# Dilated attention: the scores of both heads of a pair issued together, on the two halves of the array's rows

## The chip, the cores and the metric

The kernel runs on one core of one Trainium2 chip. Its time is the device time of one execution in microseconds (us). The core's engines are TensorE (PE; its weight loads are listed apart as PEld), VectorE (DVE), ScalarE (ACT), GpSimd (POOL) and SyncE (SP), which issues most of the DMAs.

## What is computed

Two blocks follow each other: one of two layers with two kinds of attention side by side, and one with adaptive norms, grouped attention, pooling, convolution and two mixtures of experts. The change lies in the first block, in its dilated attention: 512 tokens, 8 heads of width 64, three groups with dilations 1, 4 and 16. Shortened:

```python
DIL_PAIRS = ((128, 1), (512, 4), (2048, 16))
...
def banded_attention(q, k, v, half):
...
    s = jnp.einsum('nbqhd,nbkhd->nbhqk', qp, kw).astype(jnp.float32) * (Dh ** -0.5)
    s = jnp.where(valid[None, :, None], s, -jnp.inf)
    m = jnp.max(s, axis=-1, keepdims=True)
    e = jnp.exp(s - m)
    l = jnp.sum(e, axis=-1, keepdims=True)
    o = jnp.einsum('nbhqk,nbkhd->nbqhd', (e / l).astype(v.dtype), vw)
    lse = (m + jnp.log(l))[..., 0]
...
def dilated_attention(dil_qkv, cos, sin):
...
    alpha = jax.nn.softmax(jnp.stack(lses, axis=0), axis=0)
    out = jnp.einsum('gbsh,gbshd->bshd', alpha, jnp.stack(outs, axis=0).astype(jnp.float32))
```

The weighting of the three groups by their log-sums makes this the same as one softmax over all keys of the three groups. The kernel uses that: a row of 512 scores holds 256 columns of group 0 and 128 each of groups 1 and 2, and a mask takes out what doesn't count.

## The kernel before

The first block (`block1_layer`, L451) runs twice, for layers L = 0 and 1. Its attention is cut into 64 **units** per layer, a unit being one head and one quarter of 128 queries: units 0 to 31 are the 8 latent heads ("MLA"), units 32 to 63 the 8 dilated heads, four units to a head. So there are 32 dilated units in each layer, 64 in all, and two heads make a pair of 8 units. `unit(u)` (L892) issues, in this order on PE: `scores(u)`; at every eighth unit `values` of the pair before (L851); and `transposed(u - 2)` (L837), which turns the probabilities of two units ago.

`scores(u)` (L802) takes one PSUM bank from the pool "s", which has two. For a dilated unit it issues four matmuls at L824, each with 64 contraction rows and 32 output partitions (`tile_position=(e * 64, 32 * j)`), and two at L830 and L831 with 64 rows and 128 output partitions. `e` is the head within its pair: head 0 of a pair has its queries and keys on partitions 0 to 63, head 1 on partitions 64 to 127 of the same tiles. All of these are float32, for which the trace shows two matmul records each. Then DVE adds the mask and takes the row minimum (L833, into a `pr` tile, of which there are three), ACT takes the exponential with its sum (L795), and DVE takes the reciprocal and scales (L797, L798). `transposed` brings the result through PE (L844) into a `PT` tile, and `values` multiplies it with V for both heads of the pair, on the two halves of the output partitions (L859 for MLA, L865 and L874 for dilated heads).

Between the units stands other work, the **fill**: `weave` (L440) deals a list of steps out over the eight units of a window by costs that are written beside them. The lists are `fills` (L903); windows 4 to 7 hold the dilated units:

```python
        qk_[1] + gate(1, 1) + wout(1),
        qk_[2] + v1[4:12],
        qk_[3] + ctx[0:2] + w2[0:2] + gate(1, 2),
        w2[2:3] + gate(1, 3) + ctx[2:4] + w2[3:4],
```

A fill step of the projection kind is 24 matmuls of 128x512 (L350 to L352: each product in three terms) whose weights come by DMA, are rounded by ACT (L401) and get their remainder from DVE (L402). Windows 4 to 6 have about one such step per unit. Window 7 has few, so that several units follow each other with nothing between them. `qk_[hp]` are the projections of the pair's queries and keys: each evacuated by ACT (keys at L569), a few rows sent by DMA to be rotated on DVE (L590 to L599) and sent back by GpSimd's DMAs (L601). `wout` adds an output projection into x (L668), `gate` is evacuated at L648 and L649. Beside all this runs the table work of the second block, on DVE alone (L967 and L968), with weights by DMA.

The order on PE and SP is the order of the program; that on DVE, ACT and POOL is set by a scheduler.

Of the kernel before, what the change touches and what calls it, by code (L numbers as in the profile page):

```python
# [21 lines left out]
P = 128  # L22
# [248 lines left out]
class K:  # L271
# [17 lines left out]
    def t(self, shape, tag, bufs, dt=F32):  # L289

        pool = self.sb if tag in ("wraw", "whi", "wlo", "cath", "catl") else self.two if tag == "big" else self.of.get(tag, self.pool)
        return pool.tile(shape, dt, tag=tag, bufs=bufs, name=self.nm(tag))
# [158 lines left out]
def block1_layer(k, L, x, hT):  # L451
    nc, I, t, fm = k.nc, k.I, k.t, k.fm
# [249 lines left out]
    cats, vss, qks, gates, mq, cT, vm = {}, {}, {}, {}, {}, [], []  # L702
# [89 lines left out]
    def softmax(pr, bias, src):  # L792

        l = t([P, 1], "l", 4)
        nc.scalar.activation(pr, src, AF.Exp, scale=-1.0, bias=bias, accum_out=l)  # L795
        rl = t([P, 1], "rl", 4)
        nc.vector.reciprocal(rl, l)  # L797
        nc.vector.tensor_scalar(pr, pr, rl, None, op0=ALU.mult)  # L798

    heads = [Head() for _ in range(16)]  # L800

    def scores(u):  # L802
        h, i = u // 4, u % 4
        hd = heads[h]
        dil, hh = h // 8, h % 8
        e = hh % 2
        rows = slice(e * 64, e * 64 + 64)
        if i == 0:
            hd.pr = {}
        sp = k.bank("s")  # L810
        mn = t([P, 1], "mn", 4)
        cs = slice(i * P, (i + 1) * P)
        if not dil:
            q, kt = mq[hh]
            nc.tensor.matmul(sp, q[:, cs], kt, start=True, stop=True)
            pr = t([P, 512], "pr", 3)
            nc.vector.tensor_reduce(mn, sp, AX.X, ALU.min)
            softmax(pr, mn, sp)
        else:
            qs = qks[hh // 2]  # L820
            q0, q1, q2 = (qs[(0, g)] for g in range(3))
            k0, k1, k2 = (qs[(1, g)] for g in range(3))
            for j in range(4):
                nc.tensor.matmul(  # L824
                    sp[32 * j : 32 * j + 32, 0:256],
                    q0[rows, i * P + 32 * j : i * P + 32 * j + 32],
                    k0[rows, P * j : P * j + 256],
                    start=True, stop=True, tile_position=(e * 64, 32 * j),
                )
            nc.tensor.matmul(sp[:, 256:384], q1[rows, cs], k1[rows, cs], start=True, stop=True)  # L830
            nc.tensor.matmul(sp[:, 384:512], q2[rows, cs], k2[rows, cs], start=True, stop=True)  # L831
            pr = t([P, 512], "pr", 3)
            nc.vector.tensor_tensor_reduce(pr, sp, k.dil_mask[:, i, :], 1.0, 3e38, ALU.add, ALU.min, mn)  # L833
            softmax(pr, mn, pr)
        hd.pr[i] = pr

    def transposed(u):  # L837
        h, i = u // 4, u % 4
        hd = heads[h]
        if i == 0:  # L840
            hd.PT = t([P, 4, 512], "PT", 2)
        pt = k.bank("pt")
        for j in range(4):
            nc.tensor.transpose(pt[:, j * P : (j + 1) * P], hd.pr[i][:, j * P : (j + 1) * P], ident)  # L844
        if h < 8:
            dst = hd.PT[:, :, i * P : (i + 1) * P]
        else:
            dst = hd.PT[:, i, :].rearrange("p (j q) -> p j q", j=4)
        k.copy(dst, pt.rearrange("p (j q) -> p j q", j=4))
# [42 lines left out]
    def unit(u):  # L892
        if u < 64:
            scores(u)
        if u >= 10 and u % 8 == 2:
            values(u // 8 - 1)
        if 2 <= u < 66:
            transposed(u - 2)
# [1090 lines left out]
def body(tc, I, out, stop=None):  # L1989
    nc = tc.nc  # L1990
    with (
# [21 lines left out]
        with k.phase("two"):  # L2013
            k.two = k.pool
            with tc.manual_schedule(engines={mybir.EngineType.PE, mybir.EngineType.SP}):
# [27 lines left out]
                for L in range(2):  # L2043
                    block1_layer(k, L, x, hT)
                    k.late = None
# [37 lines left out]
```

## Time and profile before

| | |
|---|---|
| three runs | 1874.26, 1878.16, 1883.65 us; median 1878.16 us |
| profiled execution | 1880.58 us, of which the span is 1878.8 us |
| PE busy | 1739.2 us (93%) |
| DVE busy | 1350.5 us (72%) |
| ACT busy | 772.9 us (41%) |
| POOL busy | 279.5 us (15%) |
| dilated units in time | first layer 253.7 to 490 us, second layer 758.8 to 992 us from the span's start |
| mean granted clock of PE over the span | 0.96 |

Shares are of the span. Matmul records overlap, since the next one starts before the last has ended: the time that a group of matmuls takes on PE is read from start to start of what follows, not from the sum of its durations.

### The profile page before, as it was taken

What the parts mean: (1) busy time and instruction counts of PE and PEld (TensorE: products, weight loads), DVE (VectorE), ACT (ScalarE), POOL (GpSimd) and SP (SyncE); (2) the same over time, 40 slices, a digit from 0 to 9 for tenths busy, and PEclk for the clock granted to TensorE, in tenths of its full rate; (3) what the DMA queues carried; (4) which work ended last, traced back from release to release, by engine and by line L of the source; (5) the groups of instructions that cost most, each with busy time, mean ns of one, the idle gap of its engine ahead of it and who ended that gap; (6) DMA issues with size and microseconds to landing.
All of it is one profiled execution on the core that took longest, in us unless ns stands there. A gap on an engine that the chain in (4) does not pass through costs nothing. (4 is left out here: it accounts for less than half of the span.)

```text
span 1878.8 us, 25737 instructions
## 1 busy us (share of the span) xinstructions
PE 1739.2 (93%) x9542; PEld 1346.2 (72%) x9542; DVE 1350.5 (72%) x2532; ACT 772.9 (41%) x1345; POOL 279.5 (15%) x242
## 2 busy tenths in 40 slices
PE   7999999999899999999997879996999799969996
PEld 6877777787697767778776857774666587846663
DVE  4577778876546777576566797879887775689874
ACT  4444333334343533333424445553555332135552
POOL 0000000001100000000002353013321121142221
PEclk9999999999999999999998879997999799979998
DMA  5345565654023544554412213136996463169983
GB/s 174 120 138 152 157 201 164 208 165 133 20 72 116 147 143 139 172 161 139 153 56 89 75 55 115 52 144 244 331 347 211 153 229 90 46 230 308 345 297 75
DMA packets 86948, 298.90 MB, mean 159 GB/s; under 512 B 18854, under 2 KB 20694, under 8 KB 78624
## 3 DMA queue, kind: packets, MB, share of 16 engines
q1 hardware_dynamic: 71584, 271.87, 43.8%
q0 software_dynamic: 10704, 19.79, 4.6%
q10 hardware_dynamic: 4528, 5.51, 1.1%
q8 instruction: 78, 1.28, 0.3%
q14 instruction: 54, 0.44, 0.1%
HBM read 280.23 MB, written 24.96 MB: 162 GB/s over the span
## 5 line engine op out<-in xcount | busy, mean ns | idle before, releaser
L401 ACT ACTIVATE whi<-wraw 128x1024 fp32r<-128x1024 f32 (+2 forms) x166 | 171.8, 1037 | 356.7 <-PE psmm L351 240.3
L402 DVE TENSOR_TENSOR wlo<-wraw,whi 128x1024 fp32r<-128x1024 f32 (+3 forms) x165 | 200.9, 1219 | 133.7 <-ACT whi L401 121.0
L350 PE MATMUL psmm<-big,whi 128*128 128x512 f32 x672 | 271.6, 404 | 0.8 <-ACT e L1265 0.8
L351 PE MATMUL psmm<-big,whi 128*128 128x512 f32 x672 | 265.8, 396 | 0.0
L352 PE MATMUL psmm<-big,wlo 128*128 128x512 f32 x672 | 265.6, 395 | 0.0
L968 DVE CUSTOM_DVE_ANT_0 wraw<-wraw,sB 128x1024 f32<-128x1024 f32 x96 | 117.3, 1222 | 73.1 <-DMA wraw<-in_mw_dram 72.6
L350 PE MATMUL psmm<-whi,big 128*128 128x256 f32 (+2 forms) x496 | 165.3, 333 | 1.0 <-ACT big L401 1.0
L351 PE MATMUL psmm<-wlo,big 128*128 128x256 f32 (+2 forms) x496 | 160.7, 324 | 4.7 <-DVE wlo L402 4.7
L352 PE MATMUL psmm<-whi,big 128*128 128x256 f32 (+2 forms) x496 | 160.1, 323 | 2.4 <-DVE big L402 2.3
L352 PEld LDWEIGHTS psmm<-big,wlo 128*128 128x128 f32 x672 | 126.4, 188 | 30.8
L350 PEld LDWEIGHTS psmm<-big,whi 128*128 128x128 f32 x672 | 126.6, 188 | 29.2 <-ACT e L1265 1.0
L351 PEld LDWEIGHTS psmm<-big,whi 128*128 128x128 f32 x672 | 126.7, 189 | 27.8
L1853 PE MATMUL psmm<-wraw,hs 128*128 128x512 f32 x256 | 121.9, 618 | 5.5 <-ACT hs L1845 3.5
L601 POOL DMA_DIRECT2D qk<-rope x40 | 20.4, 512 | 677.9 <-DVE rope L599 239.7
L351 PEld LDWEIGHTS psmm<-wlo,big 128*128 128x128 f32 x496 | 112.2, 226 | 5.8 <-DVE wlo L402 5.6
L352 PEld LDWEIGHTS psmm<-whi,big 128*128 128x128 f32 x496 | 111.5, 225 | 3.2 <-DVE big L402 3.2
L350 PEld LDWEIGHTS psmm<-whi,big 128*128 128x128 f32 x496 | 111.7, 225 | 2.0 <-ACT big L401 1.6
L350 PE MATMUL pss<-whi,xTh 128*128 128x512 f32 x256 | 104.7, 409 | 2.3 <-ACT xTh L401 2.3
L352 PE MATMUL pss<-whi,xTl 128*128 128x512 f32 x256 | 102.2, 399 | 1.7 <-DVE xTl L402 1.7
L351 PE MATMUL pss<-wlo,xTh 128*128 128x512 f32 x256 | 103.3, 404 | 0.0
L844 PEld LDWEIGHTS pspt<-c_ident,pr 128*128 128x128 f32 x512 | 59.3, 143 | 48.4 <-issue 25.5
L402 DVE TENSOR_TENSOR wlo<-bigm,whi 128x1024 fp32r<-128x1024 f32 x64 | 78.0, 1223 | 17.7 <-ACT whi L401 16.2
(386 smaller groups left out, 3733.1 us busy)
## 6 DMA issues: line engine op xcount, KB each, us to landing
wraw<-in_mw_dram SPq DMA_DIRECT2D x96, 512.0 KB, 4.0
big<-in_me_dram SPq DMA_DIRECT2D x32, 1024.0 KB, 9.1
bigm<-in_me_dram SPq DMA_DIRECT2D x32, 1024.0 KB, 6.6
wraw<-in_me_dram SPq DMA_DIRECT2D x64, 512.0 KB, 7.6
wraw<-in_wqk_dram SPq DMA_DIRECT2D x48, 512.0 KB, 3.8
wraw<-in_wv_dram SPq DMA_DIRECT2D x24, 512.0 KB, 4.1
wraw<-in_ow_dram SPq DMA_DIRECT2D x20, 512.0 KB, 3.6
wraw<-in_wg_dram SPq DMA_DIRECT2D x16, 512.0 KB, 3.6
```

Source lines behind the costliest of these rows:

```text
L350: mm(out, lhs[0], rhs[0], start=first, stop=False)
L351: mm(out, lhs[0], rhs[1], start=False, stop=False)
L352: mm(out, lhs[1], rhs[0], start=False, stop=last)
L401: self.nc.scalar.activation(hi, src, AF.Copy)
L402: (sub or self.nc.vector).tensor_tensor(lo, src, hi.bitcast(F32), ALU.subtract)
L601: nc.gpsimd.dma_start(tiles[b][48:80, :], R[b // 4][32 * (b % 4) : 32 * (b % 4) + 32, :])
L844: nc.tensor.transpose(pt[:, j * P : (j + 1) * P], hd.pr[i][:, j * P : (j + 1) * P], ident)
L968: nc.vector.tensor_tensor_reduce(w, w, sB, 1.0, 0.0, ALU.mult, ALU.add, mf[:, j : j + 1])
L1853: nc.tensor.matmul(acc, hs[:, c * P : (c + 1) * P], w[:, c * 512 : (c + 1) * 512], start=c == 0, stop=c == 1)
```

## The change

For the dilated units the order of the units within a pair of heads changes, and the scores of two units are issued as one group. `place(u)` now alternates the heads: the even unit is head 0 of the pair, the odd unit head 1, for the same quarter of the queries. At the even unit `dilated` takes both banks of the pool "s" and issues the matmuls of both heads in turn, head 0 on rows 0 to 63 into one bank, head 1 on rows 64 to 127 into the other. The odd unit issues no score matmuls. Mask, softmax, transposes, values and fill stay with their units. The MLA units are as before.

```diff
+    def place(u):
+
+        return (u // 4, u % 4) if u < 32 else (u // 8 * 2 + u % 2, u % 8 // 2)
+
+    banks = {}
+
+    def dilated(hp, i):
+
+        qs = qks[hp]
+        cs = slice(i * P, (i + 1) * P)
+        pair = [(k.bank("s"), slice(e * 64, e * 64 + 64)) for e in range(2)]
+        for j in range(4):
+            for sp, rows in pair:
+                nc.tensor.matmul(
+                    sp[32 * j : 32 * j + 32, 0:256],
+                    qs[(0, 0)][rows, i * P + 32 * j : i * P + 32 * j + 32],
+                    qs[(1, 0)][rows, P * j : P * j + 256],
+                    start=True, stop=True, tile_position=(rows.start, 32 * j),
+                )
+        for g in (1, 2):
+            for sp, rows in pair:
+                nc.tensor.matmul(sp[:, (g + 1) * P : (g + 2) * P], qs[(0, g)][rows, cs], qs[(1, g)][rows, cs], start=True, stop=True)
+        return [sp for sp, _ in pair]
+
     def scores(u):
-        h, i = u // 4, u % 4
+        h, i = place(u)
...
-            for j in range(4):
-                nc.tensor.matmul(
-                    sp[32 * j : 32 * j + 32, 0:256],
-                    q0[rows, i * P + 32 * j : i * P + 32 * j + 32],
-                    k0[rows, P * j : P * j + 256],
-                    start=True, stop=True, tile_position=(e * 64, 32 * j),
-                )
-            nc.tensor.matmul(sp[:, 256:384], q1[rows, cs], k1[rows, cs], start=True, stop=True)
-            nc.tensor.matmul(sp[:, 384:512], q2[rows, cs], k2[rows, cs], start=True, stop=True)
+            if h % 2 == 0:
+                banks[0], banks[1] = dilated(hh // 2, i)
+            sp = banks[h % 2]
...
     def transposed(u):
-        h, i = u // 4, u % 4
+        h, i = place(u)
```

Lines behind the new functions are 12 higher after the change: L844 becomes L856, L833 becomes L845. The score matmuls of the dilated heads are at L815 (32 output partitions) and L823 (128).

PE's order, before, at the first two dilated units of the first layer (`pss` is a score bank, `psmm` a bank of the fill, `pspt` one of the transposes; the 24 fill matmuls between the units are left out):

```order
L352 MATMUL psmm_2207<-big_77,wlo_2201 128x512
L824 MATMUL pss_2235<-k_443_2032,qk_1538 32x256 x4
L830 MATMUL pss_2235<-qk_1910,qk_1620 128x128
L831 MATMUL pss_2235<-qk_1979,qk_1857 128x128
L844 MATMUL pspt_2250<-c_ident,pr_2154 128x128 x4
...
L824 MATMUL pss_2297<-k_443_2032,qk_1538 32x256 x4
L830 MATMUL pss_2297<-qk_1910,qk_1620 128x128
L831 MATMUL pss_2297<-qk_1979,qk_1857 128x128
L844 MATMUL pspt_2312<-c_ident,pr_2185 128x128 x4
```

PE's order, after, at the same place:

```order
L815 MATMUL pss_2236<-k_443_2032,qk_1538 32x256
L815 MATMUL pss_2237<-k_443_2032,qk_1538 32x256
L815 MATMUL pss_2236<-k_443_2032,qk_1538 32x256
L815 MATMUL pss_2237<-k_443_2032,qk_1538 32x256
...
L823 MATMUL pss_2236<-qk_1910,qk_1620 128x128
L823 MATMUL pss_2237<-qk_1910,qk_1620 128x128
L823 MATMUL pss_2236<-qk_1979,qk_1857 128x128
L823 MATMUL pss_2237<-qk_1979,qk_1857 128x128
L856 MATMUL pspt_2257<-c_ident,pr_2154 128x128 x4
...
L856 MATMUL pspt_2312<-c_ident,pr_2185 128x128 x4
```

The scores of the second unit have moved ahead by one unit, past the transposes and the fill of the first, and stand matmul by matmul between those of the first; the second unit has only its transposes left.

DVE's order, before, at the same two units (`mn` is the row minimum, `wraw` the raw weights of the table work and of the fill):

```order
L833 ISA pr_2243,mn_2236<-pss_2235,dil_mask 128x512
L833 ISA mn_2236 128x1
L649 SCALAR_TENSOR_TENSOR gc_2232<-gc_2232,psmm_2207 128x512
L368 COPY PT_2161<-pspt_2250 128x4x128
L797 RECIPROCAL rl_2247<-l_2245 128x1
...
L833 ISA pr_2305,mn_2298<-pss_2297,dil_mask 128x512
L833 ISA mn_2298 128x1
```

DVE's order, after:

```order
L845 ISA pr_2250,mn_2235<-pss_2236,dil_mask 128x512
L845 ISA mn_2235 128x1
L368 COPY PT_2161<-pspt_2257 128x4x128
L845 ISA pr_2305,mn_2304<-pss_2237,dil_mask 128x512
L845 ISA mn_2304 128x1
L797 RECIPROCAL rl_2254<-l_2252 128x1
```

The mask step of the second unit, which frees the second bank, has moved up to just behind that of the first.

## Rows read from the trace of the kernel before

**Rows 1.** The page's first lines: span, and busy time of each engine.

```profile
span 1878.8 us, 25737 instructions
PE 1739.2 (93%) x9542; PEld 1346.2 (72%) x9542; DVE 1350.5 (72%) x2532; ACT 772.9 (41%) x1345; POOL 279.5 (15%) x242
```

**Rows 2.** Busy time by stretch: dilated units, windows 4 to 6 and 7, each layer.

```profile
core 0: us, PE busy (x) PEld busy (x) DVE busy (x) ACT busy (x) POOL busy (x), PEclk, DMA share, GB/s
253.00:461.00 208.00, 206.68 (x1232) 158.67 (x1234) 161.11 (x295) 73.26 (x122) 15.22 (x26) 1.00 0.59 177
461.00:490.00 29.00, 26.65 (x230) 18.96 (x230) 18.25 (x44) 10.79 (x24) 0.57 (x1) 0.98 0.18 48
758.00:965.00 207.00, 206.25 (x1227) 158.81 (x1226) 133.82 (x257) 70.23 (x121) 10.33 (x23) 1.00 0.50 146
965.00:992.00 27.00, 26.12 (x226) 18.33 (x224) 15.58 (x36) 10.76 (x22) 0.00 (x0) 1.00 0.08 21
```

**Rows 3.** Timeline of PE at a dilated unit: start, us, instruction, [idle before].

```profile
260.52 0.40 PE L351 MATMUL psmm<-big,whi 128*128 128x512 f32 x1
260.75 0.39 PE L352 MATMUL psmm<-big,wlo 128*128 128x512 f32 x1
261.07 0.64 PE L824 MATMUL pss<-k,qk 64*32 64x256 f32 x8
261.64 0.49 PE L830 MATMUL pss<-qk,qk 64*128 64x128 f32 x2
261.96 0.38 PE L831 MATMUL pss<-qk,qk 64*128 64x128 f32 x2
262.28 0.65 PE L844 MATMUL pspt<-c_ident,pr 128*128 128x128 f32 x4
```

**Rows 4.** Score matmuls of all dilated units: count, ns min/median/max, starts; idle before them.

```profile
L824 PE MATMUL pss<-k,qk x512: 372/376/400, 253.7 to 990.1; 64*32 64x256 f32 x171
L830 PE MATMUL pss<-qk,qk x128: 272/322/373, 254.3 to 990.6; 64*128 64x128 f32 x128
L831 PE MATMUL pss<-qk,qk x128: 272/272/272, 254.6 to 990.8; 64*128 64x128 f32 x128
...
  DMA k<-rope: 1.1, 1
```

**Rows 5.** PE timeline: first four column tiles of a unit; the next unit; values on column halves.

```profile
261.07 0.42 PE L824 MATMUL pss<-k,qk 64*32 64x256 f32 x4
...
268.47 0.64 PE L824 MATMUL pss<-k,qk 64*32 64x256 f32 x8
...
269.67 3.65 PE L859 MATMUL psav<-PT,v 128*64 128x512 f32 x16
...
468.48 1.97 PE L865 MATMUL psav<-PT,v 128*64 128x128 f32 x32
```

**Rows 6.** DVE by line, 253 to 461 us: busy us, mean ns, idle before it.

```profile
L968 DVE CUSTOM_DVE_ANT_0 wraw<-wraw,sB 128x1024 f32<-128x1024 f32 x31 | 37.9, 1222 | 19.0 <-DMA wraw<-in_mw_dram 18.7
L402 DVE TENSOR_TENSOR wlo<-wraw,whi 128x1024 fp32r<-128x1024 f32 x26 | 31.8, 1222 | 11.8 <-ACT whi L401 11.8
```

**Rows 7.** Keys of the dilated heads, first layer: evacuations; timeline of POOL and PE.

```profile
L569 ACT ACTIVATE k<-psmm x4: 579/580/587, 231.9 to 445.9; 128x512 f32<-128x512 f32 x4
...
458.71 0.50 POOL L601 DMA_DIRECT2D k<-rope  x1
...
460.93 0.64 PE L824 MATMUL pss<-k,qk 64*32 64x256 f32 x8 [1.14 <-DMA k<-rope]
```

**Rows 8.** Timeline at the end of the first layer's units, DVE and PE.

```profile
486.57 0.69 DVE L833 CUSTOM_DVE_ANT_0 pr<-pss,dil_mask 128x512 f32<-128x512 f32 x1
...
489.73 1.94 PE L844 MATMUL pspt<-c_ident,pr 128*128 128x128 f32 x8 [2.20 <-DVE pr L798]
```

**Rows 9.** Timeline at the end of the second layer's units, DVE.

```profile
988.97 0.69 DVE L833 CUSTOM_DVE_ANT_0 pr<-pss,dil_mask 128x512 f32<-128x512 f32 x1
...
991.40 0.69 DVE L833 CUSTOM_DVE_ANT_0 pr<-pss,dil_mask 128x512 f32<-128x512 f32 x1
```

More of the change, by code (lines that the diff above doesn't have):

```diff
@@ L800, in block1_layer @@
     heads = [Head() for _ in range(16)]
+    def place(u):
[17 more added lines that the diff above has]
+        return [sp for sp, _ in pair]
     def scores(u):
-        h, i = u // 4, u % 4
+        h, i = place(u)
         hd = heads[h]
         dil, hh = h // 8, h % 8
-        e = hh % 2
-        rows = slice(e * 64, e * 64 + 64)
         if i == 0:
             hd.pr = {}
-        sp = k.bank("s")
         mn = t([P, 1], "mn", 4)
-        cs = slice(i * P, (i + 1) * P)
         if not dil:
+            sp = k.bank("s")
             q, kt = mq[hh]
-            nc.tensor.matmul(sp, q[:, cs], kt, start=True, stop=True)
+            nc.tensor.matmul(sp, q[:, i * P : (i + 1) * P], kt, start=True, stop=True)
             pr = t([P, 512], "pr", 3)
@@ L819, in scores @@
         else:
-            qs = qks[hh // 2]
-            q0, q1, q2 = (qs[(0, g)] for g in range(3))
-            k0, k1, k2 = (qs[(1, g)] for g in range(3))
-            for j in range(4):
-                nc.tensor.matmul(
-                    sp[32 * j : 32 * j + 32, 0:256],
-                    q0[rows, i * P + 32 * j : i * P + 32 * j + 32],
-                    k0[rows, P * j : P * j + 256],
-                    start=True, stop=True, tile_position=(e * 64, 32 * j),
-                )
-            nc.tensor.matmul(sp[:, 256:384], q1[rows, cs], k1[rows, cs], start=True, stop=True)
-            nc.tensor.matmul(sp[:, 384:512], q2[rows, cs], k2[rows, cs], start=True, stop=True)
+            if h % 2 == 0:
+                banks[0], banks[1] = dilated(hh // 2, i)
+            sp = banks[h % 2]
             pr = t([P, 512], "pr", 3)
```

## The prediction

> **What bounds the kernel now.** I began with the page's totals: PE is busy for 1739.2 of 1878.8 us [rows 1]. An average over a span proves little, so next I took the stretches in which the changed code runs. In windows 4 to 6 PE is busy for 206.68 of 208 us in the first layer and 206.25 of 207 us in the second, at a granted clock of 1.00 (the upper of its two levels), while DVE has 161.11 and 133.82 us and ACT about 70 [rows 2]. The reader is to see that PE is full there and the next engine is not: a microsecond of PE work removed in these stretches should come off the end. In window 7 PE is still at 26.65 of 29 and 26.12 of 27 us, but the units follow each other closely, so a chain through DVE may take over.
>
> Then the timeline of one unit, to see how long its scores hold PE [rows 3]. The scores begin at 261.07 and the transposes behind them at 262.28: **1.21 us a unit**. That isn't streaming time. Eight records of L824 lie within 0.64 us though each lasts 0.376; the two groups that follow have four records, 0.11 us apart at best (two of L831 within 0.38 us, each 0.272). Most of the rest is waiting at two seams: 0.57 us from the first L824 to L830, and 0.32 us from the first L831 to the transposes. Entering costs something too: the last fill matmul starts 0.32 us ahead of the scores, where fill matmuls start 0.23 us apart, so 0.09 us more. All 64 dilated units look like this: the records of each line have nearly the same minimum, median and maximum over 512, 128 and 128 matmuls [rows 4]. The next unit starts 7.40 us later, so scores are 1.21 of each 7.40 us [rows 3, 5].
>
> **The change, part by part.** No score matmul is added or removed: 8 + 2 + 2 records per unit stay. They are grouped in twos, so 32 groups replace 64.
>
> *Two units before:* 2 x 1.21 + 0.09 for the second entry = 2.51 us. The second unit's transposes will now follow the fill directly, and I take nothing for that.
>
> *One group after:* unknown, because no row shows matmuls on two row halves next to each other. From below: both halves run side by side. The nearest rows are of column tiles. The first four column tiles of a unit, each 0.400 us, all lie within 0.42 us, so they start 0.007 us apart and do run side by side [rows 5]. The values matmuls alternate between two column halves: 32 records of 128 columns take 1.97 us and 16 of 512 columns 3.65 us [rows 5], where one after the other, 0.11 us apart per 128 columns as at L831 [rows 3], they would take 3.5 and 7.0 us. They go two at a time. If row halves do the same, the group is as long as one unit plus a few starts, 1.21 + 0.04 = 1.25 us, and a pair of units gains 2.51 - 1.25 = 1.26, taken as **1.25 us**. From above, as long as the order of column tiles holds: the second half adds its own 0.5 us of column tiles (0.26 from first to last start, and the step of 0.24 to the next) and 4 x 0.11 = 0.44 us, so 1.21 + 0.94 = 2.15 us and a gain of 0.36. Farther out, each L824 matmul of the mixed order runs alone; that is the slow rival. I take the lower bound, because the two halves read different partitions, write different banks, and are as independent as the column halves that the trace shows in twos.
>
> The Trainium skill (TensorEngine Tiling (Array Packing), Key Properties) says that different tiles can load weights and multiply in parallel, and that changing the tiling mode, not the tile alone, drains the engine; by that rule the seams of rows 3 are paid once a group and the gain is the 1.25 us. Its page TensorE: Matmul & The Clock Gate (Part 3) gives 3.07 times for four row tiles, short of four; two tiles at that efficiency, as an estimate, would make the group 2.41/1.53 = 1.6 us and the total about 1854. No row here shows either.
>
> *Where it counts.* Each of windows 4 to 6 has four groups, so 12 in each layer.
> - First layer, windows 4 to 6: window 7 begins with a wait of 1.14 us for the rotated keys. They left PE's banks at 445.9, within the last two units of window 6, and their DMA is issued at 458.71 [rows 7]; this chain doesn't get shorter, so what the last group saves is waited out. 11 x 1.25 = 13.75 us.
> - Second layer, the same windows: the wait for keys occurs once in both layers together [rows 4]; 12 x 1.25 = 15.0 us.
> - Window 7 of each layer has four groups. Three gain 1.25. But a group needs both score banks, and the mask step of the odd unit before it must have freed the second. In windows 4 to 6 the mask steps now stand one behind the other on DVE, a unit of 7 us ahead, so nothing waits. In window 7, where two groups have only values and transposes between them, the odd unit's mask step (0.69 us [rows 8]) needs the `pr` tile that the transposes two units back let go, and PE has only one set of transposes (four records within 0.65 us [rows 3]) to cover it and its signals: I charge 0.5 us once in each layer. 2 x (3.75 - 0.5) = 6.5 us.
> - The last group. In the first layer the last transposes wait 2.20 us for DVE [rows 8], and DVE starts from the fill before, so PE's saving is swallowed: 0. In the second, three mask steps stand in a row behind the last fill, 988.97 to 991.40, about 1.2 us each with what lies between [rows 9]; two remain: 1.25 us.
>
> Sum: 13.75 + 15.0 + 6.5 + 1.25 = **36.5 us**, as much as 29.2 groups in full. Against the profiled execution that is 1880.58 - 36.5 = 1844; that execution stood 2.4 us above the median of 1878.16, so I forecast **1842 us**, 1.9% faster. Costed at nothing: masks, softmax, transposes and copies, which are the same in number and lie under PE's 7 us of fill; without that cover (window 7) they are charged above. Next in line, if PE gives way, is the DVE of the first layer.
>
> **The rivals.**
> - *Weight loads in line.* The halves multiply side by side, but the 128-column weights load one after the other. Column halves can't tell, since a load of 64 columns is half as long. Then the second half's four records add 4 x 0.11 us: a group of 1.69, a gain of 0.82 x 29.2 = 24 us, **1854**.
> - *Halves one after the other* (the change doesn't do what it says): the upper bound of 2.15, only seams saved, 0.36 x 29.2 = 10.5 us, **1868**. For it: no row shows two row halves at once. Against it: rows 5.
> - *DVE takes over in the first layer.* There DVE is busy 161.11 us and idles 19.0 us ahead of the table work, for its weights, and 11.8 us for ACT [rows 2, 6]. If none of that shrinks, 161 + 31 = 192 us is what windows 4 to 6 need, hardly below the 208 - 13.75 = 194 of my forecast; any new stall on DVE, or its order, would give back up to the 13.75 us: **1856**. Against it: ACT waits for PE there, so that part shrinks with PE. The skill's page on tiling (PSUM Bottleneck) names this way out, that tiling doesn't speed up the emptying of banks; by it the time is that of this rival.
> - *Slower: the alternation breaks the column tiles.* If two matmuls on different row halves aren't taken together, e0, e1, e0, e1 means that no two neighbours run side by side. Then 8 matmuls of L815 take two steps of 0.24 us each, 3.84 us in place of 0.48, and the second half adds 0.44 as above: 1.21 + 3.36 + 0.44 = 5.0 us, 2.5 us more than two units before. 32 x 2.5 = 80 us, **1958**. It turns slower from a group of 2.51 us. For it: the order puts every second matmul on the other half. Against it: L859 alternates in just this way between column halves and keeps its twos.
> - *The gain is lost behind*: chains after each layer (norm, weights) don't start earlier. Little speaks for it, as those waits hang on the units' own ends. **1878**.
>
> **How the numbers follow.** Forecast 0.64, with its own range of 1835 to 1849 for the small terms and the spread of the runs; weight loads 0.13; halves in turn 0.07; DVE 0.06; slower 0.05; lost 0.05. A measurement here can tell about 0.5% from no change, 9.4 us, so faster means below 1868.8. Faster: 0.64 + 0.13 + 0.06 + half of 0.07 = 0.86; same: 0.05 + the other half = 0.09; slower 0.05. The range takes in the forecast, the weight loads and DVE, 0.83 in all, with some room: 1832 to 1862.
>
> **What would show it.** In the changed profile a group should hold PE for about 1.25 us from its first L815 to the L856 behind it (1.7: weight loads in line; 2.15: halves in turn; 5: the alternation breaks). The stretches of windows 4 to 6 should shrink by some 14 and 15 us at the same fill. A wait of PE for keys at the first layer's window 7 should be about 2.3 us. Short waits for DVE should stand before a group in window 7 alone. I am wrong if PE shows waits for L845 in windows 4 to 6, if DVE is busy there for over 95%, or if a group is over 2 us.

## The result, and the profile after

The changed kernel takes **1857.26 us** (median of 4 runs, 1853.23 to 1861.11); the kernel before, on the same chip, 1877.49 (4 runs, 1874.26 to 1883.65). The ratio is 0.9888, 95% interval 0.9854 to 0.9922. It is faster by some 20 us: inside the range, in the foretold direction, and little more than half of the 36.5 us of the sum. The profiled execution took 1858.75 us. Its page begins:

```profile
span 1857.0 us, 25754 instructions
PE 1705.9 (92%) x9542; PEld 1334.2 (72%) x9542; DVE 1346.4 (73%) x2532; ACT 770.8 (42%) x1345; POOL 278.2 (15%) x242
```

PE has 33 us less work than in [rows 1], with as many instructions; DVE, ACT and POOL have what they had. The span fell by only 21.8 us. So most of the foretold 36.5 us of PE work went away, and some 11.5 us of it came back as idle time.

First the group itself, PE's timeline at a pair of units in the first layer (start, us, instruction):

```profile
322.43 0.39 PE L352 MATMUL psmm<-whi,catl 128*128 128x512 f32 x1
322.75 0.66 PE L815 MATMUL pss<-k,qk 64*32 64x256 f32 x16
323.34 0.71 PE L823 MATMUL pss<-qk,qk 64*128 64x128 f32 x8
323.99 0.66 PE L856 MATMUL pspt<-c_ident,pr 128*128 128x128 f32 x4
...
330.09 0.60 PE L856 MATMUL pspt<-c_ident,pr 128*128 128x128 f32 x4
```

Sixteen records of L815 begin within the time in which eight did in [rows 3]. From the first to the transposes it is 323.99 - 322.75 = 1.24 us, for two units, where one took 1.21. All 32 groups are like this, but for one in each window 7, which last 2.37 and 1.68 us; in the first of them the trace shows a wait of 0.52 us for a mask step (L845). The second unit has only transposes (330.09).

Then the stretches of [rows 2], cut at the new times (same columns: us, PE, PEld, DVE, ACT and POOL busy, PE's granted clock, DMA):

```profile
253.00:456.00 203.00, 195.19 (x1228) 154.79 (x1226) 160.73 (x295) 71.36 (x121) 16.00 (x26) 0.97 0.59 184
456.00:481.00 25.00, 21.84 (x229) 16.43 (x228) 16.57 (x41) 11.25 (x23) 0.00 (x0) 1.00 0.13 35
748.00:948.00 200.00, 194.09 (x1228) 154.38 (x1226) 132.61 (x257) 69.75 (x121) 10.44 (x23) 0.98 0.50 151
948.00:972.00 24.00, 22.58 (x236) 17.05 (x235) 16.52 (x41) 11.39 (x24) 0.00 (x0) 1.00 0.08 24
```

Where PE idled for 1.3 and 0.75 us in [rows 2], it now idles for 7.8 and 5.9 us, and its granted clock is no longer 1.00. What it waited for, windows 4 to 7 of the first layer and then of the second (us in total, times, longest):

```profile
PE psmm L350 <- DVE x L668: 4.2, 2, 4.0
PE psmm L350 <- DVE gc L649: 3.3, 1, 3.3
PE pspt L856 <- DVE pr L798: 3.0, 1, 3.0
PE pss L815 <- DVE mn L845: 0.5, 1, 0.5
...
PE psmm L350 <- DVE gc L649: 2.7, 1, 2.7
PE psmm L350 <- DVE x L668: 1.6, 1, 1.6
...
PE psmm L351 <- DVE wlo L402: 1.1, 1, 1.1
```

The new ones are those of `psmm`: the fill wants one of its three banks, and DVE hasn't emptied it (L649, a gate; L668, the addition of an output projection). The keys' wait of [rows 7] is gone.

What DVE does ahead of the longest of the first kind, after:

```profile
305.35 0.72 DVE L590 STREAM_SHUFFLE rope<-rope 64x512 f32<-64x512 f32 x1
306.11 1.22 DVE L979 CUSTOM_DVE_ANT_0 v<-wraw,v 128x1024 f32<-128x1024 f32 x1
307.26 0.08 DVE L979 DVE_READ_ACCUMULATOR2_ANT modc<- 128x1 f32 x1
307.26 3.27 DVE L598 TENSOR_TENSOR rope<-rope,v 32x512 f32<-32x512 f32 x4
310.56 0.69 DVE L649 SCALAR_TENSOR_TENSOR gc<-gc,psmm 128x512 f32<-128x512 f32 x1
```

and PE, which has a wait there and then matmuls 0.43 us apart:

```profile
311.30 0.80 PE L350 MATMUL psmm<-whi,cath 128*128 128x512 f32 x1 [3.33 <-DVE gc L649]
311.90 0.63 PE L351 MATMUL psmm<-wlo,cath 128*128 128x512 f32 x1
312.32 0.63 PE L352 MATMUL psmm<-whi,catl 128*128 128x512 f32 x1
```

The same place before, DVE and PE:

```profile
306.73 3.35 DVE L598 TENSOR_TENSOR rope<-rope,v 32x512 f32<-32x512 f32 x4
310.11 0.49 DVE L798 TENSOR_SCALAR pr<-pr,rl 128x512 f32<-128x512 f32 x1
310.51 0.68 DVE L599 TENSOR_TENSOR rope<-rope,rope 64x512 f32<-64x512 f32 x1
311.12 0.67 DVE L649 SCALAR_TENSOR_TENSOR gc<-gc,psmm 128x512 f32<-128x512 f32 x1
...
311.84 0.50 PE L350 MATMUL psmm<-whi,cath 128*128 128x512 f32 x1
```

The gate was emptied half a microsecond *later* there than now, and PE got to its next matmul just as it ended. PE is now ready for it at 311.30 - 3.33 = 307.97, 3.9 us ahead of the start before; DVE isn't. What PE has saved is waited out, and then PE's clock is at the lower of its two levels (1.2 GHz) for a while: 0.51 granted from 310 to 317 us, where 12 fill matmuls go 0.43 us apart and no longer 0.23.

Averages over the stretches hide this. DVE is busy 161 of 208 us in [rows 2]; the piece around this place, before and then after (same columns as above):

```profile
291.00:325.00 34.00, 33.82 (x187) 24.48 (x186) 32.73 (x62) 11.68 (x19) 3.23 (x8) 1.00 0.49 144
```

```profile
288.00:321.00 33.00, 29.67 (x162) 22.67 (x161) 31.36 (x60) 8.86 (x16) 3.23 (x8) 0.90 0.43 133
```

DVE is busy 32.73 of 34 us (96%) before as well, beside a PE that is full. Both engines were full at once there; only PE was made faster.

The other long waits have more than a full DVE behind them. Ahead of the wait of 3.96 us at 448.82, one of the four multiplications took 3.07 us while GpSimd computed the remainder of a weight (L402) beside it, so that the four took 5.31 us and not 3.27:

```profile
442.64 5.31 DVE L598 TENSOR_TENSOR rope<-rope,v 32x512 f32<-32x512 f32 x4
443.59 2.51 POOL L402 TENSOR_TENSOR v<-wraw,v 128x1008 fp32r<-128x1008 f32 x1 [5.16 <-ACT v L401]
```

The same GpSimd step lay beside them before the change too, where they took 4.76 us and PE waited for no fill bank. And ahead of the wait of 2.66 us in the second layer, DVE was not full: it stood idle for 3.07 us, by the trace for the weights of a table step, and then its order put that step and the rotation ahead of the gate:

```profile
797.89 1.23 DVE L980 CUSTOM_DVE_ANT_0 wraw<-wraw,sB 128x1024 f32<-128x1024 f32 x1 [3.07 <-DMA wraw<-in_mw_dram]
799.81 3.37 DVE L598 TENSOR_TENSOR rope<-rope,v 32x512 f32<-32x512 f32 x4
804.95 0.67 DVE L649 SCALAR_TENSOR_TENSOR gc<-gc,psmm 128x512 f32<-128x512 f32 x1
```

### The profile page after: what moved, and what is told of

It reads as the page before. It is cut to its first block, busy times and chain, and to the rows that moved or that the text cites. A ratio compares the mean times of both kernels' runs of the same rounds, so it can differ in the third digit from the quotient of the medians.

```text
span 1857.0 us, 25754 instructions
## 1 busy us (share of the span) xinstructions
PE 1705.9 (92%) x9542; PEld 1334.2 (72%) x9542; DVE 1346.4 (73%) x2532; ACT 770.8 (42%) x1345; POOL 278.2 (15%) x242
## 3 DMA queue, kind: packets, MB, share of 16 engines
q8 instruction: 78, 1.28, 0.3%
## 5 line engine op out<-in xcount | busy, mean ns | idle before, releaser
L401 ACT ACTIVATE whi<-wraw 128x1024 fp32r<-128x1024 f32 (+2 forms) x166 | 171.7, 1036 | 348.1 <-PE psmm L351 241.6
L402 DVE TENSOR_TENSOR wlo<-wraw,whi 128x1024 fp32r<-128x1024 f32 (+3 forms) x165 | 200.9, 1219 | 102.3 <-ACT whi L401 89.6
L856 PEld LDWEIGHTS pspt<-c_ident,pr 128*128 128x128 f32 x512 | 61.3, 143 | 48.2 <-issue 28.9
L402 DVE TENSOR_TENSOR wlo<-bigm,whi 128x1024 fp32r<-128x1024 f32 x64 | 77.9, 1223 | 17.7 <-ACT whi L401 16.2
```

The lines of the kernel that those rows point to most:

```text
L401: self.nc.scalar.activation(hi, src, AF.Copy)
L402: (sub or self.nc.vector).tensor_tensor(lo, src, hi.bitcast(F32), ALU.subtract)
```

## The experiments

**Theory A**, from these rows: in windows 4 to 6 DVE's rotation of queries and keys (L590 to L599, with L598 alone 3.3 us), with table work among it, stood hidden under PE's slower units. Now it is late, PE waits for a fill bank, and the clock falls behind the wait. **Rivals**: the pairing of the score banks makes PE wait (Theory B below); the clock falls by itself (Theory C); the new order of the units costs the time (Rival D). Number 3 asks something else, whether the two halves run side by side only because their matmuls alternate.

**1. The rotation's second step left out.** The kernel leaves out the multiplications of L598, so its queries and keys differ; their values take another path through the experts at the end (1536 matmuls at L1905, on a path that the changed kernel doesn't enter), and its total (4298.81 us) says nothing. Only the stretch up to the end of the dilated units is read.

```diff
-                    for sl, perm in ((slice(0, 32), "p (r l) -> p r l"), (slice(32, 64), "p (r l) -> p l r")):
...
-                            nc.vector.tensor_tensor(d, d, dil_cs[sl, c, :].rearrange(perm, r=4), ALU.mult)
+                    pass
```

> The changed kernel, with the four multiplications of the second rotation step (L598, 4 x 0.82 us of DVE for each pair of heads) left out, so keys and queries of that step are not rotated. Theory A (PE, now ahead, waits for banks of the fill that DVE empties too late, since the rotation stands ahead of the gate's and the output projection's steps in DVE's order, and PE's clock halves after each such wait): the waits of 3.3, 4.0, 2.7 and 1.6 us shrink to under 1 us each, the stretches at half clock behind them go, and of the 17 us lost most come back: 1840 us, 1837 to 1847. Theory B (the two score banks taken together cost the time): nothing changes but the shorter DVE time, 1857. Theory C (the clock falls by itself): the waits go, the half-clock stretches stay, 1846.

PE's waits in windows 4 to 6 of the first layer, and the longest in those of the second:

```profile
PE psmm L350 <- DVE x L665: 0.2, 1, 0.2
...
PE psmm L351 <- DVE wlo L402: 0.4, 1, 0.4
```

No stretch of lower clock is left in either. As a marker behind the units of the second layer I take the second set of four transposes at L414: it starts at 950.65 us, where it is 971.82 in the changed kernel and 994.06 before. So without that work on DVE the dilated windows gain 21 us more, though PE has the same instructions. The clock doesn't fall by itself, and pairing the banks isn't the cause: the groups are still there. But all of L598 went, 11.9 us of DVE's time in the first layer's windows 4 to 6, so it doesn't say what a smaller cut is worth.

**2. The new order alone.** Heads alternate, each unit issues its own scores.

```diff
-        pair = [(k.bank("s"), slice(e * 64, e * 64 + 64)) for e in range(2)]
+        pair = [(k.bank("s"), slice(e * 64, e * 64 + 64))]
...
+            sp = dilated(hh // 2, i, h % 2)
```

> The units of the two heads alternate as in the changed kernel, but each unit issues its own scores, 64 groups of one head as before. Theory A: PE is as slow as before the change, 1.21 us a unit, DVE keeps up, no wait for a bank of the fill over 0.6 us in the dilated windows, 1877 us (1872 to 1882). Rival D (the new order of the units, by the order that the scheduler then gives DVE, causes the waits): waits of 2.7 to 4 us as in the changed kernel, and a time of 1888 or more.

1881.51 us beside 1881.07 of the kernel before, ratio 1.0005 (0.9994 to 1.0017). A unit's scores take 1.21 us as before, and the longest wait for a fill bank is 0.3 us. The order costs nothing; the waits come with the shorter scores.

**3. One half after the other.** The group stays, but all matmuls of head 0 are issued ahead of those of head 1.

```diff
-        for j in range(4):
-            for sp, rows in pair:
+        for sp, rows in pair:
+            for j in range(4):
```

> The changed kernel with the group in another order: all six matmuls' records of head 0 of a kind first, then those of head 1 (four column tiles of head 0, four of head 1, two of head 0, two of head 1). If PE starts matmuls in the program's order and puts only what stands near side by side: the second half's first column tile waits for the first half's last, some 0.25 us, and the four records of each half at the wide matmuls go 0.11 us apart in turn, 0.35 to 0.44 more; a group of 1.8 us and some 0.6 x 29 = 17 us over the changed kernel, 1874. If halves run side by side in any order: a group of 1.24 us and 1857.

```profile
255.22 0.66 PE L815 MATMUL pss<-k,qk 64*32 64x256 f32 x16
255.81 0.72 PE L823 MATMUL pss<-qk,qk 64*128 64x128 f32 x8
256.47 0.33 PE L856 MATMUL pspt<-c_ident,pr 128*128 128x128 f32 x1
```

The group takes 1.25 us, as in the change, and the kernel 1856.46 us, ratio 0.9878 (0.9859 to 0.9896). What I had expected of this order was wrong: the halves run side by side however they are interleaved, so the gain comes from issuing both within one group.

**4. Fill banks first.** DVE is to prefer the gate and the addition to the rotation.

```diff
+            with k.tc.high_priority():
                 nc.vector.scalar_tensor_tensor(sg, sg, 1.0, acc, op0=ALU.add, op1=ALU.mult)
...
+                with k.tc.high_priority():
                     nc.vector.tensor_tensor(xs, acc, xs, ALU.add)
```

> The changed kernel, with the gate's two steps (ACT and DVE) and the output projection's add on DVE at high priority for the scheduler; in DVE's order the gate's step moves up past three of the four L598 multiplications. Nothing is left out. Theory A: the waits of PE shrink by some 2.5 us each, and part of the half-clock stretches go: 1847 us, 1840 to 1852. Theory B or D: 1857.

1855.38 us, ratio 0.987 (0.9851 to 0.9888), some 8 us above what was expected. PE's two longest waits in the first layer's windows 4 to 6 and at the first scores of window 7:

```profile
PE pss L817 <- DMA k<-rope: 6.3, 1, 6.3
PE psmm L350 <- DVE x L670: 1.7, 1, 1.7
```

The waits for banks shrank, and the rotation, pushed back, made the keys late: 6.3 us at window 7. Both chains run through the same DVE, and order alone only trades one wait for the other.

**5. Half of the rotation's second step on GpSimd.**

```diff
-                            nc.vector.tensor_tensor(d, d, dil_cs[sl, c, :].rearrange(perm, r=4), ALU.mult)
+                            (nc.gpsimd if c else nc.vector).tensor_tensor(d, d, dil_cs[sl, c, :].rearrange(perm, r=4), ALU.mult)
```

> The change, with two of the four multiplications of the rotation's second step (L598, c = 1) moved from VectorE to GpSimd, so that VectorE reaches the emptying of TensorE's fill banks (L649, L668) about 1.6 us sooner in each block. Theory A (VectorE's rotation block, no longer covered, makes TensorE wait for a fill bank): the waits of 3.33 and 3.96 us of the first layer and 2.66 and 1.63 us of the second become about 1.7, 2.3, 1.0 and 0; some 6.4 us of waiting less, and one or two of the half-clock stretches with them: 1848 us (1844 to 1852). Rival G: GpSimd slows VectorE's own multiplications while it runs (they took about 1.25 us in place of 0.82 when GpSimd subtracted beside them), so that little is saved: waits within 0.7 us of what they were, 1855 to 1859.

1860.49 us, ratio 0.9891 (0.9861 to 0.9921): nothing gained. DVE and POOL at the place that was shown above:

```profile
306.02 4.20 POOL L598 TENSOR_TENSOR rope<-rope,v 32x512 f32<-32x512 f32 x2 [3.21 <-DVE rope L590]
...
307.09 4.03 DVE L598 TENSOR_TENSOR rope<-rope,v 32x512 f32<-32x512 f32 x2
```

Two multiplications on DVE took 4.03 us beside two on POOL, where four on DVE alone took 3.27. Rival G holds: the block didn't shrink, and PE's wait was 4.23 us. The Trainium skill (SBUF — State Buffer, "SBUF: two separate sides") says that VectorE and GpSimd take turns at a shared pair of ports, whole instructions at a time, when VectorE reads both its inputs from SBUF and GpSimd reads SBUF as well. The trace agrees: GpSimd's shortest multiplication in this run took 1.27 us, so that two of them and the two of VectorE, one after the other, would need some 4.2 us; from 306.02 to 311.12 the four took 5.1.

**6. Table work moved by one window.** In the first layer window 4 carries two steps of the table work per weight tile; here window 5 does.

```diff
-        k.rate = (1, 1, 1, 1, 2 - L, 1, 1, 0)[w]
+        k.rate = (1, 1, 1, 1, 1, 2 - L, 1, 0)[w]
```

> The change, with the table work's double rate in the first layer moved from the fifth window of units to the sixth, so that one L979/L980 pair less stands among VectorE's rotation work at 305 to 312 us. Theory A: the wait of 3.33 us at 311.30 shrinks to under 1.5 us and its half-clock stretch goes, 4 to 6 us less in the first layer; the second layer is as in the change: about 1852 us. Rival: the table work is not part of what VectorE is late by (the rotation alone makes it late), or the next window's bank now waits in its place: 1857 us.

1864.88 us, ratio 0.9935 (0.9906 to 0.9964), slower than the change by the medians, though the two intervals touch. The wait of 3.33 us became 0.8, and two others came in window 5. PE's waits in the first layer's windows 4 to 6:

```profile
PE psmm L350 <- DVE x L668: 5.0, 3, 4.0
PE pss L815 <- DVE mn L845: 3.8, 1, 3.8
PE psmm L351 <- DVE wlo L402: 3.5, 1, 3.5
PE psmm L350 <- DVE gc L649: 0.8, 1, 0.8
```

So the table work is part of what makes DVE late in window 4, and window 5 has no room for it: by the trace window 4 holds 10 table steps here and not 13, window 5 holds 17 and not 12.

The second layer of this run is as in the change and has the same two waits of 2.66 and 1.63 us, but the granted clock stays at 1.00 behind the first (811 to 816 us). Its window 4 is 2.86 us shorter than in the change (65.77 in place of 68.63) and its window 5 is 1.77 us longer (73.23 in place of 71.46), in one execution of each. So in this pair of executions sparing the lower clock was worth 1.1 us over the two windows, and not 2.9.

**7 and 8. The fill reordered; then edits 5, 6 and 7 together.**

```diff
-        qk_[2] + v1[4:12],
-        qk_[3] + ctx[0:2] + w2[0:2] + gate(1, 2),
+        qk_[2][0:2] + gate(1, 2) + qk_[2][2:6] + v1[4:8],
+        qk_[3] + v1[8:12] + ctx[0:2] + w2[0:2],
```

> The change, with the order of the fill altered in windows 5 and 6 alone: what follows the rotation of the keys in window 6 is emptied by ScalarE (v1) and no longer by VectorE (gate), and the gate's step stands behind the first two steps of the queries in window 5. No work is added or taken out. Theory A: the waits for L668 at 448.82 (3.96 us) and 942.37 (1.63 us) and the half-clock stretch at 450.1 go, 6 to 8 us less: 1850 us; the waits for L649 in window 4 (3.33 and 2.66 us) stay. If the rotation's chain to the keys is what bounds the end of window 6, the time appears as a wait of the first scores of window 7 for the keys, and the total is 1855 to 1858 us.

> The three edits together: two rotation multiplications on GpSimd, the table work's rate moved by one window, the fill of windows 5 and 6 reordered. Theory A: no wait for a fill bank over 1.5 us in windows 4 to 6 of either layer, no half-clock stretch there, 13 to 15 us less than the change: 1843 us (1840 to 1848), that is near the forecast. If the waits move on to the keys of window 7 or to other banks: 1850 us or more.

The reordering gave 1859.6 us, ratio 0.9888 (0.9864 to 0.9911), no different from the change: the waits for L668 went, and others of 1.2 to 2.1 us, for L625 and for converted weights (L401, L402), took their places. All three together gave 1873.07, ratio 0.9963 (0.9946 to 0.9981): waits of 4.7, 3.6 and 3.4 us in the first layer. Beside POOL's multiplications a table step of DVE takes twice its 1.22 us:

```profile
307.14 2.44 DVE L980 CUSTOM_DVE_ANT_0 wraw<-wraw,sB 128x1024 f32<-128x1024 f32 x1
```

Five ways of moving DVE's work (4 to 8) gained nothing. None of them made DVE's time less: it is busy for 1345.1 to 1349.4 us in these five, and for 1346.4 in the change.

**9 and 10. Less work for DVE, in the change and in the kernel before.** The second step's multiplications are four of 32 partitions because half of them read the table in another order of tokens. A second constant table in that order lets two of 64 partitions do the same arithmetic, for one more load per pair of heads.

```diff
+    c["dil_cs2"] = np.ascontiguousarray(np.stack([np.concatenate([g[:, cl], g]) for g in (grp_c, grp_s)], axis=1))
...
+            dil_cs2 = t([P, 2, 512], "v4", 10)
+            nc.sync.dma_start(dil_cs2[:64], I["dil_cs2"])
...
-                    for sl, perm in ((slice(0, 32), "p (r l) -> p r l"), (slice(32, 64), "p (r l) -> p l r")):
-                        for dst, c in ((R[j], 0), (rs, 1)):
-                            d = dst[sl].rearrange("p (a b) -> p a b", a=4 if perm.endswith("r l") else P)
-                            nc.vector.tensor_tensor(d, d, dil_cs[sl, c, :].rearrange(perm, r=4), ALU.mult)
+                    for dst, c in ((R[j], 0), (rs, 1)):
+                        nc.vector.tensor_tensor(dst[:64], dst[:64], dil_cs2[:64, c, :], ALU.mult)
```

> The change, with the rotation's second step made shorter on VectorE and nothing put beside it: a second constant table in that step's order of tokens, so that two multiplications over 64 partitions (about 0.68 us each, as L599 over 64) replace four over 32 (3.27 us in all); one more table load of 256 KB per pair. VectorE saves 1.9 us per block, 15 us over the eight blocks. Theory A (TensorE waits for fill banks behind VectorE's rotation block): the waits of 3.33 and 2.66 us for L649 become about 1.4 and 0.7, those of 3.96 and 1.63 for L668 about 2 and 0, one or two of the half-clock stretches go with them: 1848 us (1843 to 1852). Rival K (at the end of window 6 the chain from the rotation to the keys bounds it, whatever VectorE is spared): the waits in windows 6 stay or turn into waits for the keys, 1853 us.

> The kernel before, with the same shorter rotation step. Theory A: there TensorE's own work hides VectorE's block, so VectorE's 15 us buy nothing in windows 4 to 6, at most the wait for keys of 1.14 us at window 7: within 0.2% of before, 1876 to 1882 us. Rival T (VectorE's total work sets the time of these windows in both kernels): 1865 us.

With the change: **1841.8 us**, ratio to the kernel before 0.9803 (0.9782 to 0.9823), better than expected. Without the change: 1875.07 us, ratio 0.9976 (0.9964 to 0.9988), just below what was expected. Waits, first of the new table with the change (first layer, windows 4 to 7; lines are 1 higher behind the table, so L669 is the addition L668), then of DVE's block and PE at window 7 in it, then the one wait of the kernel before with the table:

```profile
PE pspt L857 <- DVE pr L799: 3.3, 2, 3.0
PE psmm L351 <- DVE x L669: 1.0, 2, 0.8
```

```profile
307.09 1.28 DVE L599 TENSOR_TENSOR rope<-rope,v 64x512 f32<-64x512 f32 x2
308.30 0.68 DVE L650 SCALAR_TENSOR_TENSOR gc<-gc,psmm 128x512 f32<-128x512 f32 x1
...
446.65 0.66 PE L816 MATMUL pss<-k,qk 64*32 64x256 f32 x16
```

```profile
PE pspt L845 <- DVE pr L799: 2.2, 1, 2.2
```

DVE is now busy for 1330.2 us, 16 less than in the change. The block's multiplications take 1.28 us in place of 3.27, L650 comes 2.3 us earlier, the wait of 3.33 us is gone but for one of 0.76 us for an addition (311.44), that of 3.96 is gone, and no stretch of lower clock is left in windows 4 to 6. Window 7 begins at 446.65 with no wait for keys: rival K falls. That the same cut gives the kernel before some 5 us, part of it the 1.14 us of [rows 7] and the rest spread, and the change about 15, is what Theory A says and rival T doesn't.

The four kernels by stretch, in us. Windows 4 to 6 go from the first dilated score to the first of window 7; window 7 from there to the transposes that wait for the last unit's mask (first layer, as in [rows 8]) or to the marker of number 1 (second layer):

| | before | change | before, new table | change, new table | forecast gain | gain, old table | gain, new table |
|---|---|---|---|---|---|---|---|
| first layer, 4 to 6 | 207.24 | 202.36 | 205.24 | 191.83 | 13.75 | 4.88 | 13.41 |
| first layer, 7 | 28.80 | 25.26 | 28.78 | 25.28 | 3.25 | 3.54 | 3.50 |
| second layer, 4 to 6 | 206.54 | 199.35 | 205.24 | 192.06 | 15.0 | 7.19 | 13.18 |
| second layer, 7 | 28.74 | 23.66 | 28.73 | 23.62 | 4.5 | 5.08 | 5.11 |
| sum | 471.32 | 450.63 | 467.99 | 432.79 | 36.5 | 20.7 | 35.2 |

Where DVE isn't in the way, the change is worth 35.2 us in these stretches and 33.3 by the medians, close to the forecast.

**11. The new table, with less of the second block's table work in the dilated windows.** Windows 4 to 6 hold 24 and 7 steps of it in place of 31 and 18.

```diff
-        k.rate = (1, 1, 1, 1, 2 - L, 1, 1, 0)[w]
+        k.rate = (2, 1, 2, 1, 1, 1, 1 - L, 0)[w]
```

> The change with the shorter rotation step and with the table work taken out of the dilated windows: doubled in windows 0 and 2 of both layers, single in the first layer's window 4, none in the second layer's window 6 (the same steps in all). Theory A: the remaining waits for L649 and L668 shrink below 1 us in windows 4 of both layers, no half-clock stretch there: 1843 us (1838 to 1848). If the table work makes windows 0 and 2 wait in their place, or the keys bound the end of window 6: 1850 to 1857 us.

1842.64 us, ratio 0.98 (0.978 to 0.982): the same as number 9. The longest waits for a fill bank are 1.2 and 1.1 us, no shorter than the 0.8 and 0.7 of number 9. There was nothing to win there this way, and PE now waits 1.5 and 1.6 us for DVE at 112 and 132 us, where the work went.

## Why the prediction was right, and where its sum was wrong

The direction and the working of the group came true. That the total lies inside the range is in part luck: the forecast of 1842 us with its own range of 1835 to 1849 missed, and 1857 was inside because the range had been widened for rivals at 1854 and 1856, one of which the trace refutes and the other of which had the wrong price.

*The group*: foretold 1.25 us, measured 1.24 in the change and 1.25 in the other order. The lower bound by the column tiles of [rows 5] was the right one. Weight loads in line (1.69), halves in turn (2.15) and the broken alternation (5.0) are refuted by this number, and so is the estimate of 1.6 us that I had worked out from the Trainium skill's figure for four row tiles (TensorE: Matmul & The Clock Gate, Part 3): here two halves cost what one does. That estimate was also added up wrongly: a group of 1.6 us would have gained 0.91 x 29.2 = 27 us and given about 1852, not 1854. That the second unit's transposes cost nothing when they follow the fill directly came true (329.86 to 330.09, the 0.23 us of a fill matmul).

*Window 7 and the last group*: foretold 3.25 and 4.5 us, measured 3.54 and 5.08. The charges for mask steps, 0.5 us in each layer, came to 1.13 and 0.44: by so much the one long group of each window 7 exceeds 1.24 us. The gains come out above the forecast all the same; what made up for it is not worked out here.

*Windows 4 to 6*: foretold 13.75 and 15.0 us, measured 4.88 and 7.19. **This is the step that failed**: that PE is full there and the next engine is not, so that "a microsecond of PE work removed in these stretches should come off the end", and with it the sentence that masks, softmax, transposes and copies cost nothing because they "lie under PE's 7 us of fill". I had asked what the change's own steps hide under, and not what else on DVE had been hidden under PE's slower units: the rotation and the table work. What stood in its place are the waits for L649 and L668. The price of the loss can be read off. Against the change with the new table the first layer's stretch is 10.5 us longer: 6.6 us of it is waits (3.33 + 3.96 + 0.28 + 0.25 against 0.76 + 0.24 + 0.25), and the rest is the lower clock: 2.6 us behind 311.30, where PE takes 5.83 us to 317.13 for what takes about 3.25 at the upper level, and 1.6 behind 448.82 (8 matmuls, 0.20 us more each); these terms are estimates and add up to 10.8. The second layer's is 7.3 longer: 4.8 us of waits (2.66 + 1.63 + 0.49 + 1.12 against 0.74 + 0.38) and an estimated 2.8 of clock behind 805.68, of which, by number 6, only a part might come back.

*The rival "DVE takes over in the first layer"* was the right mechanism with the wrong place and price. It named DVE and, by chance, gave 1856 us; but I worked it out from totals, 161 + 31 us of a 208 us stretch, and had it decide only at 192 us. It decides at single places: in window 4 of the first layer within a piece of 34 us, in window 6 where GpSimd slows DVE, and in the second layer, where DVE's total is only 134 of 207 us, behind 3.07 us in which DVE was idle. There it is the order of DVE's work, the rotation ahead of the gate, and not its load. The signs that I had named against myself, waits for L845 in windows 4 to 6 and DVE over 95% busy there, didn't show: the waits were for L649 and L668, and over the whole stretch DVE was busy for 160.73 of 203 us. The Trainium skill's rule that I had cited (TensorEngine Tiling (Array Packing), PSUM Bottleneck), that tiling doesn't speed up the emptying of banks, names the kind of wait that came; but the banks here are those of the fill, not those of the tiles.

*The keys at window 7*: foretold a wait of 2.3 us, measured none, in the change (PE comes late) and in the change with the new table (446.65). I had taken the keys' times as fixed; they leave PE's banks earlier when PE is earlier, and the rotation then follows at DVE's pace. Number 4 shows this chain as the next in line when DVE is made to put it off. With it the last group of the first layer isn't swallowed, so that 12 and not 11 groups count there; 13.41 us and 1.25 us of waits that are left make 14.7, or 1.22 a group.

What stays open: how much each wait would give back by itself (the runs that removed one brought others; number 6 shows it for the lower clock alone, in one place), how much of the wait of 3.96 us is due to GpSimd's step (no run moved that step alone), and where the 5 us that the new table gives the kernel before come from, beyond the wait for keys.

## What to carry to other kernels

When an engine that is full is made faster, look at who empties its buffers, at the places where that takes longest, and not at the average of the stage. Before the change DVE was 96% busy in one piece of 34 us and 77% in the stage; its work there cost nothing only as long as PE was as slow. A busy share points to such a place but doesn't give its price: with the new table DVE is busy for 33.74 of 34 us (295 to 329 us), and PE waits only 0.76 us there. And in the second layer DVE was not full; what counts is how long its order keeps a bank. Between the last matmul into the gate's bank and the wait for it PE had two banks of six matmuls left to fill, 3 us of work (304.99 to 307.97). Then shorten the neighbour's work rather than move it: five ways of moving it gained nothing, and one that took some 2 us or more out of each block gave 15 us and brought the change to the 33 us that its own arithmetic promised.

## What the runs showed of the hardware

- The matmuls of these score groups on two row halves of the array (64 rows each, fp32, separate banks) run side by side, whether they are issued in alternation or one half after the other: 1.24 and 1.25 us for a group, 1.21 for one half.
- Behind a wait PE's granted clock can fall to the lower of its levels, and fill matmuls then start 0.43 us apart in place of 0.23. It did so behind waits of 2.66, 3.33 and 3.96 us (change), and not behind one of 1.63 us (change), one of 3.17 us (number 5) nor the same wait of 2.66 us in number 6; so these runs give no length of wait from which it falls. It cost an estimated 1.6 to 2.8 us each time in the change, on top of the wait.
- Operations that read two SBUF tensors on DVE lasted two to three times as long beside one on POOL: 2.0 us each in place of 0.82 for the rotation's multiplications (number 5), 2.44 in place of 1.22 for a table step (number 8), 3.07 us for a multiplication beside L402 in the change, where the others of its block took 0.67 to 1.02.
